# A two-layer encoder in fp32 halves: weight totals prepared by single transfers, and the first mixer weights split inside the down stage's written order

## The chip, the cores and the metric

The kernel runs on one core of one Trainium2 chip. The metric is the device time of one execution in microseconds (us). Three runs of the kernel before gave 2413.91 us as the median (2411.43 to 2414.56). The profiled execution is a fourth one and took 2415.7 us.

## The reference, cut to what matters

The input x has 512 tokens of 1024 features. Each of two layers adds half of a SwiGLU feed-forward network (FFN), then a mixer (a projection, three kinds of attention beside each other, gates, three branch projections and an output projection), then half of a second FFN. RMSNorm stands before each of the three, and once more at the end.

```python
for l in range(DEPTH):
    h = rms_norm(x, norm_g[l, 0])
    x = x + 0.5 * swiglu(h, ffn_w_gate[l, 0], ffn_w_up[l, 0], ffn_w_down[l, 0])
    h = rms_norm(x, norm_g[l, 1])
    proj = h @ w_in[l]
    ...
    x = x + merged @ w_o[l]
    h = rms_norm(x, norm_g[l, 2])
    x = x + 0.5 * swiglu(h, ffn_w_gate[l, 1], ffn_w_up[l, 1], ffn_w_down[l, 1])
return rms_norm(x, final_g)

def swiglu(h, w_gate, w_up, w_down):
    return (jax.nn.silu(h @ w_gate) * (h @ w_up)) @ w_down
```

## The kernel before, in words

**Halves.** Every fp32 operand of a matmul is split in two: a rounded high half, copied by ScalarE (ACT, `nc.scalar.copy`), and the rest, subtracted by VectorE (DVE). A product takes high by high, high by low and low by high. `weights` (L89) loads a 128x1024 weight tile over SyncE's queue (SP) into one of three `raw` buffers, splits it into one of four `whi` and `wlo` buffers, and then calls `ahead_by` (below). A `raw` buffer is free for the next load when the low half has been subtracted.

**FFN.** `ffn(l, i)` makes 22 tiles of 128 hidden features. The first ones are plain products. The other 20 run in `Seven`, which forms a block product of gate and up weights from seven half-sized products in place of eight. For this it needs sums of weight blocks, here called the weight totals: two 512 KB tiles for each of the 20 hidden tiles, `d_odd` (`t31`) and `d_even` (`t24`) in DRAM. FFN (0,0) makes what it needs on the way; for the FFNs (0,1), (1,0) and (1,1) the generator `prepare` makes them ahead of time with DMAs alone: two plain copies from ACT's queue, and three accumulating transfers from GpSimd's queue (POOL), of 512, 256 and 256 KB. That is 5 transfers per hidden tile and 100 per FFN. One step of the generator (one `yield`) issues the copies of tile k and the accumulating transfers of tiles k-2, k-4 and k-6, so up to 5 transfers at once.

**Pace.** `ahead_by(n)` adds n to a debt and takes one step of the generator for each whole unit of it. Each `weights` call adds `owed[1]`, which the stages set from `PACE`: the down stage (16 calls), the mixer's three parts (19, 22 and 25 calls). Each tile of `Seven` adds the value of `PACE["seven"]`. At its start, `ffn` calls `drained(l, i)`, which takes all steps that are still due for that FFN. `added` (L713) then reads the total of tile m, two tiles ahead of its use.

**Down stage.** `down` (L387) has eight output rows m. Rows 0 to 3 get plain products of hidden tiles 8 to 21; then four rounds j each make a seven-product of hidden tiles 0 to 7 for rows 2j and 2j+1, and plain products for row 4+j. `Operands` loads two weight rows; `first`, `second`, `third`, `fourth` split them or sums of them, `totals` and `more` make the sums on DVE. When a row is done, `advanced(m)` scales it (L491), adds it to x (L396), stores x, and lets ACT make the high half of the next norm's operand `h` (`begin`, L158); `completed(m)` makes its low half (L170) and sums the squares. The whole stage stands under `tiles.in_order()`: for each engine and queue, its instructions are chained in the order in which they are written.

**What sets the order elsewhere.** Outside of the chained blocks the framework's list scheduler orders each engine's instructions when the program is built, by readiness in its own timing and by place in the program; `tc.issue_after(ins)` adds an edge "behind this instruction in the engine's queue", without a wait. The engines run their queues in order. So the first weights of the mixer, w_qk (query and key of pair 0), then w_va, are split wherever the scheduler finds a free place in ACT's and DVE's queues between the last rows of the down stage. The mixer's first product (L119, L120, then L122) reads the eight tiles of `h` in order.

Of the kernel before, what the change touches and what calls it, by code (L numbers as in the profile page):

```python
# [2 lines left out]

# [1 line left out]

# [26 lines left out]
FOLD = 8  # L32
NO_WAIT = mybir.DependencyInfo(mybir.DependencyClass.NoSync, mybir.DependencyReason.DATA)
PACE = {
    "mixer": ((0.25, 0.45, 0.73), (0.12, 0.25, 0.43)),
    "seven": {(0, 1): 0.16, (1, 0): 0.15},
    "down": {(0, 0): 0.3, (0, 1): 0.47, (1, 0): 0.25},
}
LOW_FIRST = (2, 4, 7)
WIDE, WIDE_FIRST = frozenset((2, 3, 4, 5, 6, 7)), frozenset((3, 4, 5))  # L40
# [3 lines left out]
def encoder(ctx: ExitStack, tc: tile.TileContext, a: dict, out: bass.AP):  # L44
# [13 lines left out]
    def f(ap):  # L58
        return ap.bitcast(F32)
# [24 lines left out]


    loaded, lower, kept = [], [], []
    gbufs, whole, folded = [2 * (MF - FOLD)], {}, [True]
    prepared, ahead, due, owed, queue = {}, [], [], [0.0, 0.0], {}

    def weights(src, width=1024):  # L90
        raw = wpool.tile([P, 1024], F32, tag="raw", name="raw", bufs=3)
        hi = wpool.tile([P, 1024], F32R, tag="whi", name="whi")
        lo = wpool.tile([P, 1024], F32R, tag="wlo", name="wlo")
        for c in range(0, src.shape[-1], width):
            w = slice(c, min(c + width, src.shape[-1]))
            loaded[:] = [nc.sync.dma_start(raw[:, w], src[:, w]).ins]
            nc.scalar.copy(hi[:, w], raw[:, w])  # L97
            lower[:] = [nc.vector.tensor_tensor(out=lo[:, w], in0=raw[:, w], in1=f(hi[:, w]), op=ALU.subtract).ins]  # L98
        ahead_by(owed[1])
        return hi, lo  # L100

# [200 lines left out]
    def ffn(l, i, h, nxt=None):  # L302
# [4 lines left out]
        with tc.tile_pool(name="ffn", bufs=1) as fp, ExitStack() as order:  # L307
# [5 lines left out]
                order.enter_context(tc.issue_after(h.squared))  # L313
            else:
                sides = []
            drained(l, i)
            owed[1] = 0
            loads = []
            start, plain = (2, 4) if first else (0, 2)
# [61 lines left out]
            if nxt is None:  # L381
                finish(fp, ghi, glo, h, tiles)
                return
            owed[1] = PACE["down"].get((l, i), 0) * (1.5 if folded[0] else 1)
            down(l, i, h, nxt, fp, tiles, ghi, glo)

    def down(l, i, h, nxt, fp, tiles, ghi, glo):  # L387
# [7 lines left out]
        def add(out, in0, in1):  # L395
            nc.vector.tensor_tensor(out=out, in0=in0, in1=in1, op=ALU.add)  # L396
# [101 lines left out]
        def advanced(m):  # L498

            d, t = outs[m], xs[m]  # L500
            if m < KC - 1:
                nc.vector.scalar_tensor_tensor(
                    out=d, in0=d, scalar=-1.0 if m % 2 else 1.0, in1=banks[m], op0=ALU.mult, op1=ALU.add
                )
                scaled(d, d)
            else:
                scaled(d, banks[m])
            add(t, d, t)
            x_keep(m, t, nxt.step)
            nxt.begin(m, t)  # L510

        def squared(m):
            nxt.power(m, xs[m], lambda: fp.tile([P, S], F32, tag="sum", name="sq", bufs=2))
# [5 lines left out]
        with tiles.in_order():  # L519
# [32 lines left out]
            coming = Operands(1)  # L552
            sides.extend(folds)
            w22 = [fp.tile([P, S], F32R, tag="un", name="w22", bufs=FOLD) for _ in range(2)]
            w.first()
            w.totals()
            w.second()
            w.more()
            w.third()
            if l == i == 0:  # L560
                small_values()
            w.fourth()
            for j in range(KC // 2):
                m, last, parts = 4 + j, j == KC // 2 - 1, {}

                def begin():
                    parts[8] = split(m, 8, 8)

                def middle():
                    if j:  # L570
                        completed(2 * j - 1)
                    parts[16] = split(m, 16, 6)

                def late():
                    if not last:
                        coming.first()
                        coming.second()
                        coming.more()

                if not last:  # L580
                    coming.totals()
                added = seven(j, w, begin, middle, late)
                bank(m)
                plain(m, 8, parts[8])
                if last:
                    added()
                    advanced(2 * j)
                    squared(2 * j)
                    completed(2 * j)
                    d, t = outs[m], xs[m]  # L590
                    nc.vector.scalar_tensor_tensor(out=d, in0=d, scalar=-0.5, in1=h.rb, op0=ALU.mult, op1=ALU.mult)
                    add(t, d, t)
                    plain(m, 16, parts[16])
                    advanced(m)
                    squared(m)
                    completed(m)
                    continue
                coming.fourth()
                added()
                advanced(2 * j)  # L600
                coming.third()
                squared(2 * j)
                advanced(2 * j + 1)
                squared(2 * j + 1)
                completed(2 * j)
                plain(m, 16, parts[16])
                w, coming = coming, Operands(j + 2) if j < KC // 2 - 2 else None
# [104 lines left out]
    def added(l, i, m, fp, load=None):  # L712

        gu = a["w_gu"][l, i, m]
        with ExitStack() as order:
            if load is not None:
                order.enter_context(tc.issue_after(load))
            t = fp.tile([P, 2, S], F32, tag="sum", name="wsum", bufs=2)
            if (l, i) in prepared:
                loaded[:] = [nc.sync.dma_start(t, prepared[l, i][m][0]).ins]  # L720
                return t.rearrange("p n c -> p (n c)")
            loaded[:] = [nc.sync.dma_start(t, gu.rearrange("n p c -> p n c")[:, :, 0:S]).ins]
            t = t.rearrange("p n c -> p (n c)")
            nc.gpsimd.dma_start(t, gu[1], accum_op=ALU.add)
        return t

    def prepare(l, i):
# [5 lines left out]
        def flat(t):  # L733
            return t.rearrange("p n c -> p (n c)")
# [12 lines left out]
        for k in range(2, MF + 6):  # L747
            if k < MF:
                gu = a["w_gu"][l, i, k]
                t31, t24 = [  # L750
                    dram.tile([P, 2, S], F32, tag=f"d_{g}{l}{i}_{k}", name=f"d_{g}") for g in ("odd", "even")
                ]
                tiles[k] = t31, t24
                queued(nc.scalar.dma_start(t31, gu.rearrange("n p c -> p n c")[:, :, 0:S]))
                queued(nc.scalar.dma_start(flat(t24), gu[0]))
            if k - 2 in tiles:
                accumulate(flat(tiles[k - 2][0]), a["w_gu"][l, i, k - 2, 1])
            if k - 4 in tiles:
                t31, t24 = tiles[k - 4]
                accumulate(t24[:, 0], t31[:, 1])  # L760
            if k - 6 in tiles:
                t24 = tiles[k - 6][1]
                accumulate(t24[:, 1], t24[:, 0])
            yield

    def ahead_by(n):

# [4 lines left out]
                ahead.pop(0)  # L772
                due.pop(0)

    def drained(l, i):

        while (l, i) in due:
            if next(ahead[0], ahead) is ahead:
                ahead.pop(0)
                due.pop(0)  # L780
# [395 lines left out]
    def mixer(l, h, nxt):  # L1176
        with tc.tile_pool(name="mix", bufs=1) as mp:
# [1 line left out]


            def projected(c):
                w = weights(a["w_qk"][l, c])
                ps = mm_tile()
                product(ps, cols(w, KC), h.hi, h.lo)
                return ps
# [607 lines left out]
```

## Time and profile before

| what | before |
|---|---|
| median of three runs | 2413.91 us |
| profiled execution: its own time | 2415.7 us |
| profiled execution: span from first to last instruction | 2413.9 us |
| TensorE matmul (PE) busy | 99% |
| DVE, ACT, POOL busy | 76%, 57%, 15% |
| weight loads of PE (PEld) | 85% |
| mean granted TensorE clock | 0.996 |
| DMA traffic | 452.92 MB, mean 188 GB/s |
| chain that ended last | PE 90%, DVE 5%, DMA 2%, ACT 2%, issue 1% |

Times in the views are microseconds from the start of the span. A row of a timeline gives start, duration, engine, line and operation, output and input by name, shape, and how many instructions are merged; brackets give the idle time of the engine before it and what ended that idle time. Rows of waits give the waiting engine and line, what it waited for, then total, count and longest. The granted clock (PEclk) is 1.00 at 2.4 GHz and 0.50 at 1.2 GHz; a value between is a mean over the stretch.

### The profile page before, as it was taken

To read this page: it belongs to the slowest core of one execution; us is meant where nothing else is said; L and a number is where in the kernel's file an instruction comes from. 1 tells how busy PE (TensorE), PEld (TensorE's weight loads), DVE (VectorE), ACT (ScalarE), POOL (GpSimd) and SP (SyncE) were. 2 spreads that over 40 slices of the span, in tenths; PEclk is the share of its full clock that TensorE was granted. 3 is DMA by queue.
4 is the path that set the end of the run, shared out by engine and by line. 5 is a ranking of instruction groups with operands and counts; after the bars stand their busy time and mean duration, and the time that the engine had idled before them with its cause. 6 is when DMAs were issued, how large, how long until landed. Compare 5 with 4: busy or idle time off the path is not lost.

```text
span 2413.9 us, 35684 instructions
## 1 busy us (share of the span) xinstructions
PE 2385.9 (99%) x12954; PEld 2049.7 (85%) x12954; DVE 1832.0 (76%) x3328; ACT 1380.5 (57%) x2551; POOL 361.7 (15%) x524
## 2 busy tenths in 40 slices
PE   9999999999999999999999999999999999999998
PEld 7999888878888888887888888888888888888887
DVE  7999775756766779997889997767666666899832
ACT  6565545756666546664456664467566674566632
POOL 3100014422212110002100001143122100000000
PEclk9999999999999999999999999999999999999999
DMA  7675777687779766659556667565656824455532
GB/s 205 176 185 166 233 225 199 181 212 212 172 201 283 223 187 216 213 182 285 175 179 201 208 213 245 181 175 150 179 146 182 189 94 136 159 191 185 174 118 70
DMA packets 149777, 452.92 MB, mean 188 GB/s; under 512 B 18265, under 2 KB 23689, under 8 KB 148641
## 3 DMA queue, kind: packets, MB, share of 16 engines
q1 hardware_dynamic: 89856, 278.50, 34.7%
q0 software_dynamic: 40352, 107.36, 21.7%
q10 hardware_dynamic: 19392, 64.78, 7.5%
q8 instruction: 102, 1.67, 0.3%
q14 instruction: 75, 0.61, 0.1%
HBM read 428.52 MB, written 138.44 MB: 235 GB/s over the span
## 4 chain that ended last, share of the span: by engine, by line
PE 90%; DVE 5%; DMA 2%; ACT 2%; issue 1%; ACTq 0%; POOLq 0%; POOL 0%; DVEq 0%
PE mm L865 17%; PE mm L122 9%; PE pr L865 9%; PE mm L119 8%; PE mm L120 8%; PE plain L393 7%; PE pv L865 4%; PE mm L393 3%; PE mm L1570 2%; PE mm L1575 2%; PE mm L1571 2%; PE av L1357 2%; PE t L1347 1%; PE s L1302 1%; PE s L1303 1%; DVE wlo L106 1%
## 5 line engine op out<-in xcount | busy, mean ns | idle before, releaser
L98 DVE TENSOR_TENSOR wlo<-raw,whi 128x1024 fp32r<-128x1024 f32 x234 | 278.8, 1194 | 146.0 <-ACT whi L97 124.1
L97 ACT CAST whi<-raw 128x1024 fp32r<-128x1024 f32 x234 | 239.4, 1028 | 260.4 <-PE mm L120 89.1
L119 PE MATMUL mm<-h,whi 128*128 128x512 f32 x800 | 318.9, 399 | 4.3 <-ACT h L158 4.3
L120 PE MATMUL mm<-h,whi 128*128 128x512 f32 x800 | 314.9, 394 | 0.0
L122 PE MATMUL mm<-h,wlo 128*128 128x512 f32 x800 | 200.2, 393 | 0.6 <-DVE wlo L98 0.6
L106 DVE TENSOR_TENSOR wlo<-raw,whi 128x1024 fp32r<-128x1024 f32 x156 | 184.2, 1218 | 5.1 <-ACT whi L105 5.1
L122 PEld LDWEIGHTS mm<-h,wlo 128*128 128x128 f32 x800 | 151.8, 190 | 33.1 <-DVE wlo L98 1.0
L119 PEld LDWEIGHTS mm<-h,whi 128*128 128x128 f32 x800 | 150.4, 188 | 33.4 <-ACT h L158 5.1
L120 PEld LDWEIGHTS mm<-h,whi 128*128 128x128 f32 x800 | 150.8, 189 | 28.7
L393 PE MATMUL plain<-g,whi 128*128 128x512 f32 x672 | 162.0, 390 | 1.6 <-ACT whi L97 0.8
L105 ACT CAST whi<-raw 128x1024 fp32r<-128x1024 f32 x156 | 156.8, 1052 | 10.2 <-DMA raw<-in_w_gu 8.8
L393 PEld LDWEIGHTS plain<-g,whi 128*128 128x128 f32 x672 | 126.0, 188 | 30.3 <-DVE g L1005 1.6
L1316 ACT ACTIVATE lg<-lg,negm 128x256 f32<-128x256 f32 (+1 forms) x192 | 114.0, 594 | 27.0 <-DVE negm L1313 26.0
L105 ACT CAST whi<-wsum 128x1024 fp32r<-128x1024 f32 x90 | 94.8, 1053 | 41.5 <-PE pv L865 32.6
L984 ACT COPY gu<-mm 128x512 f32<-128x512 f32 (+1 forms) x78 | 41.9, 538 | 131.2 <-PE mm L865 131.2
L106 DVE TENSOR_TENSOR wlo<-wsum,whi 128x1024 fp32r<-128x1024 f32 x90 | 109.5, 1216 | 6.3 <-ACT whi L105 4.4
L901 DVE TENSOR_TENSOR gu<-pr,gu 128x256 f32<-128x256 f32 x234 | 98.2, 420 | 9.7 <-ACT gu L939 5.6
L67 POOL DMA_DIRECT2D x<-d_x x24 | 13.4, 558 | 561.1 <-DVE gu L901 493.7
L745 POOL DMA_DIRECT2D d_odd<-in_w_gu x60 | 51.1, 856 | 306.9 <-DMA d_odd<-in_w_gu 189.2
L1558 DVE TENSOR_TENSOR z<-mm,rb 128x512 f32<-128x512 f32 x48 | 33.1, 691 | 76.4 <-PE mm L122 76.3
L865 PEld LDWEIGHTS mm<-h,whi 128*128 128x128 f32 x624 | 83.7, 189 | 5.6 <-PE st L247 0.4
L865 PE MATMUL mm<-h,whi 128*128 128x256 f32 x624 | 86.9, 281 | 0.0
(361 smaller groups left out, 6205.7 us busy)
## 6 DMA issues: line engine op xcount, KB each, us to landing
raw<-in_w_gu SPq DMA_DIRECT2D x94, 512.0 KB, 3.4
d_odd<-in_w_gu ACTq DMA_DIRECT2D x60, 512.0 KB, 5.9
d_even<-in_w_gu ACTq DMA_DIRECT2D x60, 512.0 KB, 6.6
d_odd<-in_w_gu POOLq DMA_DIRECT2D x60, 512.0 KB, 8.9
wsum<-d_odd SPq DMA_DIRECT2D x60, 512.0 KB, 3.2
raw<-d_even SPq DMA_DIRECT2D x60, 512.0 KB, 4.4
raw<-in_w_gate SPq DMA_DIRECT2D x48, 512.0 KB, 5.3
raw<-in_w_qk SPq DMA_DIRECT2D x44, 512.0 KB, 5.1
```

Of the source, the lines that this page charges most:

```text
L97: nc.scalar.copy(hi[:, w], raw[:, w])
L98: lower[:] = [nc.vector.tensor_tensor(out=lo[:, w], in0=raw[:, w], in1=f(hi[:, w]), op=ALU.subtract).ins]
L105: nc.scalar.copy(hi, src)
L106: nc.vector.tensor_tensor(out=lo, in0=src, in1=f(hi), op=ALU.subtract)
L119: nc.tensor.matmul(ps, wh, xhi[k], start=k == 0, stop=False)
L120: nc.tensor.matmul(ps, wh, xlo[k], start=False, stop=False)
L122: nc.tensor.matmul(ps, wl, xhi[k], start=False, stop=k == n - 1)
L393: nc.tensor.matmul(ps, w, x, start=start, stop=stop, skip_group_check=True)
L745: queued(nc.gpsimd.dma_start(out, more, accum_op=ALU.add, max_dma_last_dim=4 * 1024))
L865: nc.tensor.matmul(out, wk, bk, start=go, stop=end, skip_group_check=True)
L901: nc.vector.tensor_tensor(out=out, in0=in0, in1=in1, op=ALU.add)
L1316: nc.scalar.activation(p, p, AF.Exp, bias=negm, scale=-1.0, accum_out=total)
```

## The change

**Preparing.** `prepare` yields after each single transfer, so a unit of pace is now one transfer. All values of `PACE` are new, and the down stage has two (rows 0 to 3, and the four rounds). The former factor of 1.5 in the down stage goes. `ready[l, i]` notes the last tile whose totals have been issued, and `drained(l, i, m)` moves from the start of the FFN into `added`: it takes only as many transfers as tile m still lacks.

**Seam to the mixer.** In the last round of the down stage of the first FFN of each layer (`i == 0`), the loads and splits of the two w_qk tiles are written into the chained order, behind `completed(6)`; the mixer's first two projections take them from `begun`. `completed(6)` itself moves behind two DVE instructions of row 7. `advanced` now returns its add, and in both FFNs that have a down stage the next two `weights` calls put their DVE subtraction behind the add of row 7 (`guard`).

**First round.** `w.totals()` (two DVE adds) is written ahead of `w.first()` (a split on ACT and DVE).

```diff
 PACE = {
-    "mixer": ((0.25, 0.45, 0.73), (0.12, 0.25, 0.43)),
-    "seven": {(0, 1): 0.16, (1, 0): 0.15},
-    "down": {(0, 0): 0.3, (0, 1): 0.47, (1, 0): 0.25},
+    "mixer": ((1, 1, 1.9), (0.6, 0.8, 1.2)),
+    "seven": {(0, 1): 2, (1, 0): 2},
+    "down": {(0, 0): (1, 2.75), (0, 1): (0.4, 1.5), (1, 0): (1, 2.5)},
 }
...
             nc.scalar.copy(hi[:, w], raw[:, w])
-            lower[:] = [nc.vector.tensor_tensor(out=lo[:, w], in0=raw[:, w], in1=f(hi[:, w]), op=ALU.subtract).ins]
+            with tc.issue_after(guard.pop()) if guard else nullcontext():
+                lower[:] = [nc.vector.tensor_tensor(out=lo[:, w], in0=raw[:, w], in1=f(hi[:, w]), op=ALU.subtract).ins]
...
-            drained(l, i)
             owed[1] = 0
...
-            owed[1] = PACE["down"].get((l, i), 0) * (1.5 if folded[0] else 1)
+            owed[1] = PACE["down"].get((l, i), (0, 0))[0]
...
+            w.totals()
             w.first()
-            w.totals()
             w.second()
...
             w.fourth()
+            owed[1] = PACE["down"][l, i][1]
...
                     squared(2 * j)
-                    completed(2 * j)
                     d, t = outs[m], xs[m]
                     nc.vector.scalar_tensor_tensor(out=d, in0=d, scalar=-0.5, in1=h.rb, op0=ALU.mult, op1=ALU.mult)
                     add(t, d, t)
+                    completed(2 * j)
+                    if i == 0:
+                        begun.extend(weights(a["w_qk"][l, c]) for c in range(2))
                     plain(m, 16, parts[16])
-                    advanced(m)
+                    guard[:] = 2 * [advanced(m)]
...
             if (l, i) in prepared:
+                drained(l, i, m)
                 loaded[:] = [nc.sync.dma_start(t, prepared[l, i][m][0]).ins]
...
                 queued(nc.scalar.dma_start(t31, gu.rearrange("n p c -> p n c")[:, :, 0:S]))
+                yield
                 queued(nc.scalar.dma_start(flat(t24), gu[0]))
+                yield
             if k - 2 in tiles:
                 accumulate(flat(tiles[k - 2][0]), a["w_gu"][l, i, k - 2, 1])
+                yield
             if k - 4 in tiles:
                 t31, t24 = tiles[k - 4]
                 accumulate(t24[:, 0], t31[:, 1])
+                yield
             if k - 6 in tiles:
                 t24 = tiles[k - 6][1]
                 accumulate(t24[:, 1], t24[:, 0])
-            yield
+                ready[l, i] = k - 6
+                yield
...
-        while (l, i) in due:
+        while (l, i) in due and ready.get((l, i), 0) < m:
...
-                w = weights(a["w_qk"][l, c])
+                w = begun.pop(0) if begun else weights(a["w_qk"][l, c])
```

## Rows read from the trace of the kernel before

**Rows 1.** The page, its first part: busy time, share, instructions of each engine.
```profile
PE 2385.9 (99%) x12954; PEld 2049.7 (85%) x12954; DVE 1832.0 (76%) x3328; ACT 1380.5 (57%) x2551; POOL 361.7 (15%) x524
```
**Rows 2.** Waits of PE over the whole span: total us, times, longest.
```profile
PE t L1442 <- DVE lg L1503: 4.5, 1, 4.5
PE mm L119 <- ACT h L158: 4.3, 2, 2.3
PE mm L393 <- ACT gu L468: 1.8, 1, 1.8
PE mm L393 <- DVE wlo L106: 1.5, 1, 1.5
...
PE plain L393 <- ACT whi L97: 0.8, 1, 0.8
```
**Rows 3.** Windows behind long PE waits: us, engines' busy (instructions), PEclk, DMA share, GB/s.
```profile
357.50:362.00 4.50, 4.50 (x13) 3.55 (x14) 1.30 (x2) 1.49 (x2) 0.14 (x1) 0.62 0.69 230
...
1556.30:1560.90 4.60, 4.60 (x13) 3.69 (x14) 1.34 (x2) 1.51 (x2) 0.10 (x1) 0.63 0.52 175
...
527.60:535.00 7.40, 7.40 (x25) 6.04 (x26) 2.75 (x5) 2.68 (x5) 0.00 (x0) 0.66 0.36 127
```
**Rows 4.** Timeline of DVE at the seam from down stage to mixer, layer 0.
```profile
345.11 0.69 DVE L396 TENSOR_TENSOR x<-gu,x 128x512 f32<-128x512 f32 x1
...
352.31 1.22 DVE L98 TENSOR_TENSOR wlo<-raw,whi 128x1024 fp32r<-128x1024 f32 x1
353.45 0.68 DVE L396 TENSOR_TENSOR x<-gu,x 128x512 f32<-128x512 f32 x1
354.24 0.69 DVE L491 SCALAR_TENSOR_TENSOR gu<-plain,rb 128x512 f32<-128x512 f32 x1
354.85 1.22 DVE L98 TENSOR_TENSOR wlo<-raw,whi 128x1024 fp32r<-128x1024 f32 x1
355.98 0.69 DVE L396 TENSOR_TENSOR x<-gu,x 128x512 f32<-128x512 f32 x1
```
**Rows 5.** Timeline of ACT at the same seam.
```profile
351.64 1.05 ACT L97 CAST whi<-raw 128x1024 fp32r<-128x1024 f32 x1 [0.71 <-DMA raw<-in_w_va]
...
356.70 0.72 ACT L158 ACTIVATE h<-x,ng 128x512 fp32r<-128x512 f32 x1 [4.01 <-DVE x L396]
```
**Rows 6.** Timeline of PE at the same seam.
```profile
350.29 1.52 PE L393 MATMUL plain<-g,wlo 128*128 128x512 f32 x6
351.65 0.39 PE L119 MATMUL mm<-h,whi 128*128 128x512 f32 x1
...
357.47 0.73 PE L119 MATMUL mm<-h,whi 128*128 128x512 f32 x2 [2.04 <-ACT h L158]
```
**Rows 7.** Chain of waits, down stage of FFN (0,1): start, us, what.
```profile
1089.20 12.09 DMA d_odd<-in_w_gu
...
1106.18 16.71 DMA raw<-in_w_down
```
**Rows 8.** DMA issues, same stage, 1085 to 1135: count, KB, median us to landing.
```profile
raw<-in_w_down SPq DMA_DIRECT2D x3, 512.0 KB, 16.3
```
**Rows 9.** DMA issues at the seam, 337 to 352.
```profile
raw<-in_w_va SPq DMA_DIRECT2D x3, 512.0 KB, 9.2
```
**Rows 10.** DMA issues in Seven of FFN (0,1), 1030 to 1070: no preparing transfers.
```profile
raw<-in_w_gu SPq DMA_DIRECT2D x4, 512.0 KB, 3.3
```
**Rows 11.** DMA issues in the same stage, 948 to 968: one step of five.
```profile
raw<-in_w_gu SPq DMA_DIRECT2D x2, 512.0 KB, 6.7
```
**Rows 12.** Windows of that stage, with the step and without; columns as in rows 3.
```profile
950.00:970.00 20.00, 19.48 (x120) 17.11 (x119) 17.83 (x32) 12.67 (x21) 2.51 (x3) 1.00 0.92 284
...
1030.00:1050.00 20.00, 20.00 (x126) 17.96 (x125) 19.24 (x33) 13.49 (x23) 0.00 (x0) 1.00 0.54 184
```
**Rows 13.** Timeline of PE in the stretch with the step.
```profile
965.29 1.20 PE L865 MATMUL mm<-pair,whi 128*128 128x512 f32 x4 [0.52 <-ACT gu L933]
```
**Rows 14.** Timeline of DVE in the mixer of layer 0, ahead of the long wait.
```profile
521.89 1.22 DVE L98 TENSOR_TENSOR wlo<-raw,whi 128x1024 fp32r<-128x1024 f32 x1 [9.58 <-ACT whi L97]
```

More of the change, by code (lines that the diff above doesn't have):

```diff
@@ L1 @@
 import math
-from contextlib import ExitStack, contextmanager
+from contextlib import ExitStack, contextmanager, nullcontext
 import numpy as np
@@ L86, in encoder @@
     loaded, lower, kept = [], [], []
+    begun, guard = [], []
     gbufs, whole, folded = [2 * (MF - FOLD)], {}, [True]
-    prepared, ahead, due, owed, queue = {}, [], [], [0.0, 0.0], {}
+    prepared, ready, ahead, due, owed, queue = {}, {}, [], [], [0.0, 0.0], {}
     def weights(src, width=1024):
@@ L507, in advanced @@
                 scaled(d, banks[m])
-            add(t, d, t)
+            row = nc.vector.tensor_tensor(out=t, in0=d, in1=t, op=ALU.add).ins
             x_keep(m, t, nxt.step)
             nxt.begin(m, t)
+            return row
         def squared(m):
@@ L773, in ahead_by, with drained @@
                 due.pop(0)
-    def drained(l, i):
-        while (l, i) in due:
+    def drained(l, i, m):
+        while (l, i) in due and ready.get((l, i), 0) < m:
             if next(ahead[0], ahead) is ahead:
```

## The prediction

> **What bounds the kernel now.** I read the first part of the page, then PE's waits, then the windows behind the long ones, and only then the timelines. PE is busy for 2385.9 of the span's 2413.9 us [rows 1]. The change adds and removes no matmul, so what it can win is in PE's idle time, about 28 us, and in the clock that such idle time costs. The waits say where that is [rows 2]. One transpose waits 4.5 us for a softmax. Twice, 4.3 us together, the first product of a mixer waits for `h` (L158): the seam behind the down stage, once per layer. Three waits of 1.8, 1.5 and 0.8 us stand in a down stage. The rest are short ones that the change does not touch, or the program's start.
>
> A long wait costs more than itself. Behind each seam and behind the transpose the granted clock is at its lower level of 1.2 GHz for a while, which shows as a mean below 1 [rows 3]: 0.62 over 4.50 us, 0.63 over 4.60 us, 0.66 over 7.40 us. Busy time at a mean of 0.62 does 0.62 of the work, so the loss is 0.38 x 4.50 = 1.7 us, 0.37 x 4.60 = 1.7 us and 0.34 x 7.40 = 2.5 us. PE did nothing in the wait just before each. Behind the three waits in the down stage the clock stays up.
>
> **The seams.** In layer 0 PE ends the last row at about 351.8 (350.29 + 1.52), has begun the mixer at 351.65, and stops at 355.4, until `h` of row 7 comes at 357.47: 2.04 us [rows 6]. Of that `h`, ACT waits 4.01 us for DVE's add [rows 5]. DVE shows why [rows 4]: two subtractions for mixer weights, 1.22 us each, stand among the instructions of row 7, at 352.31 and 354.85. The first one pushes the scaling (L491) to 354.24 though the row is ready at 351.8; the second stands between it and the add (355.98).
>
> With the change both are behind the add. Then the scaling can begin at 351.9, the add at about 352.6, `h` at 353.3, and it ends at 354.0 (0.69 + 0.69 + 0.72, with the small steps between). When does PE need it? The first product starts at 351.65, and seven tiles of `h` give it 14 high-weight matmuls. Six matmuls of that size start between 350.29 and 351.65 [rows 6], 0.23 us each, so 14 take 3.2 us: 354.8. The wait should go, with 0.8 us to spare. What is late next is the low half of the same tile on DVE, which a pinned subtraction of 1.22 us can precede; I leave 0.3 us per seam for it. The w_qk splits that the change moves cost nothing as long as they fit into the last row's products. On DVE they take 2.44 us, and PE's last row is behind them.
>
> Per seam: 2.04 + 1.7 in layer 0, and in layer 1 4.3 - 2.04 = 2.3 plus 1.7. Together 7.7, less 0.6: **-7.1 us**. Bounds: 0 if another late thing takes its place (first rival), -7.7.
>
> The other seam, from FFN (0,1) to FFN (1,0), has the pin too, but no long wait stands there in rows 2: 0.
>
> **The down stage of FFN (0,1).** The chain runs for 12.09 us through one preparing copy, and then for 16.71 us through one load of down weights [rows 7]; the loads of this stretch land 16.3 us after issue [rows 8], against 3.3 us for a load of the same size in a calm stretch [rows 10]. By the code, a step was due every 1/0.705 calls there, up to five transfers at once: 23 transfers in the first eight calls. After the change these calls owe 0.4 each: 4 transfers. With 19 fewer transfers the loads should land nearly as in the calm. The waits of 0.8, 1.5 and 1.8 us are all late weights in that stage, so **-4.1 us**. Bounds: -4.1 and 0. The new order of the sums and the first split helps in the same place and has nothing left to win once the rows are early; on its own I put it at 0, since DVE does the same instructions and the adds only change places with a subtraction.
>
> **Where the transfers go.** All 300 stay. My count of the debt by stage, before and after: down (0,0) 23 and 30, with 5 more in the two moved calls; mixer of layer 0 130 and 85; Seven of (0,1) 15 and 40; down (0,1) 32 and 16; Seven of (1,0) 7 and 39; down (1,0) 26 and 28, with 5 more; mixer of layer 1 67 and 52. FFN (1,0) now starts with 76 of its 100, which makes tiles up to 12 ready, and runs ahead of need by the pace of 2; the forced part of `drained` is never taken. So no total is late by the count, and the reads two tiles ahead hide the landing.
>
> The two Seven stages get denser: two transfers in each tile. A tile is about 9.8 us long, by the distance at which its rows return in the timeline. Five transfers raised the DMA share from 0.54 to 0.92 over 20 us [rows 12], which is 7.6 us of all engines, 1.5 us each. Two per tile add 3.0 us in 9.8: 0.54 + 0.31 = 0.85. There is room, but less. With the five, the weight load took 6.7 us in place of 3.3 [rows 10, 11], and PE waited 0.52 us [rows 13]. Bounds: 0, and 0.52 us in each tile that gets an accumulating transfer, which is 4 of 5 tiles, 32 in all: +16.6. Two transfers are nearer to none than to five, and in a tile where only the two copies fell PE waited for nothing; I take **+1 us**.
>
> The Trainium skill, "DMA: Bandwidth & Descriptors", section "Issuing engines are not separate DMA queues", speaks against a free gain here: transfers started from the ACT, SP and POOL queues all run on the same 16 DMA engines and interleave, so an even pace moves contention and removes none. The rise of the load's landing from 3.3 to 6.7 us agrees with it. By that rule the Seven stages pay for what the down stage gains, which is the third rival below.
>
> **The mixers.** Outside the chained blocks the scheduler's order will shift, because the preparing transfers sit elsewhere in ACT's and POOL's queues. The stall of 4.5 us in layer 0 is such an order: DVE stood 9.58 us behind one weight subtraction [rows 14], with the softmax queued behind it. It can go (-4.5 - 2.5 = -7.0) and a like one can come (+7.0). I take 0.
>
> **Sum.** -7.1 - 4.1 + 1 = -10.2. The span of 2413.9 becomes 2403.7, and the profiled execution's 2415.7 about 2405.5. That execution lay 1.8 us above the median of the runs, 2413.91; from this median the forecast is 2404. A difference under 0.2%, 4.8 us, can't be told from none.
>
> **Rivals.**
>
> *The seam stays, with another cause.* On ACT a split of w_va that waits for its load can stand ahead of row 7's `h`, as one does in the trace at 351.64 [rows 5]; the pin holds only DVE's half. There are three `raw` buffers, so the load of the second w_va tile waits until the first w_qk tile is subtracted, and that now stands behind row 6. Row 6's add ends at 345.8 [rows 4]; add 0.72 for `h`, about 0.7 for its squares on ACT, 1.05 and 1.22 for the split: 349.5. A load landing in 3.3 us [rows 10] comes at 352.8, ACT is free at 353.9 and `h` is done at 354.6: nothing lost. One that takes 9.2 us, as the w_va loads do here [rows 9], comes at 358.7, `h` at 360.5, and PE waits 5.7 us in place of 2.0. Between the ends, at 5 to 6 us, the seam costs what it costs now. Then only the down stage gains: -4.1 + 1, 2411. For it: the loads at this seam are slow, and 5 transfers fall into the two moved calls. Against: whether the scheduler puts the split first is open.
>
> *The mixer's long wait goes too.* 2404 - 7 = 2397. For it: the order that made it depends on the pace, and rows 2 show just one wait of this kind for two mixers of the same code. Against: no part of the change aims there.
>
> *The Seven stages saturate, and it gets slower.* If an accumulating transfer per tile makes the weight loads as late as five did, 32 tiles lose 0.52 us: -11.2 + 16.6, 2419. It decides from the point where the load lands near 6.7 us in the common tile. Against: 0.85 is below the 0.92 of that stretch, and the load is issued a tile ahead.
>
> *The pace does not do what it says:* transfers still bunch, since ACT's and POOL's queues are held up by other work; down (0,1) keeps its waits, and only the seams gain: 2414 - 7, 2407.
>
> **How the numbers follow.** Forecast 0.42, seam stays 0.25, mixer wait goes 0.13, Seven saturates 0.12, pace without effect 0.08. The likeliest case gives 2404, and with its own bounds 2400 to 2408. The range takes in the second and third cases with their unknown mixer order: 2394 to 2419. Faster by over 0.2% (below 2409.1): 0.42 and 0.13 almost whole, most of 0.08, less what a new wait in a mixer takes back, 0.57. Slower by over 0.2% (above 2418.7): half of the 0.12, and the seam case with a long load or a new mixer wait, 0.15. Same: 0.28.
>
> **What would show it.** PE's waits: L119 for `h` gone or below 0.5 us at both seams, with PEclk near 1 behind them; on DVE no L98 between L491 and L396 of row 7. In the down stage of FFN (0,1) the weight loads land in under 8 us and the three waits are gone. In the Seven stages the share is near 0.85 and waits of L865 sum to under 2 us. I am wrong if ACT shows an L97 waiting for w_va ahead of the last L158, if many tiles of Seven wait 0.5 us, or if a mixer has a new wait of several us.

## The result and the profile after

After the change the kernel takes 2421.4 us (median; 2418.5 to 2423.8) against 2414.1 us before in the same session: a ratio of 1.0029, 95% interval 1.0018 to 1.0040. It is slower by 7 us where 10 us less were forecast, and lies above the range. The profiled execution took 2423.0 us, its span is 2421.3 us.

The amount of work on TensorE is as before; the first part of the page of the kernel after, against [rows 1]:

```profile
PE 2387.4 (99%) x12954; PEld 2051.6 (85%) x12954; DVE 1835.0 (76%) x3328; ACT 1380.3 (57%) x2551; POOL 367.3 (15%) x524
```

So the 7 us are in waits again, and in the clock behind them. PE's waits of the kernel after (what waited for what: total us, times, longest), against [rows 2]:

```profile
PE mm L121 <- ACT h L160: 11.7, 2, 7.5
PE pr L876 <- DVE wlo L108: 4.6, 2, 4.5
PE mm L876 <- ACT gu L944: 3.1, 6, 1.5
PE mm L1082 <- ACT whi L1041: 1.7, 1, 1.7
```

The waits for the softmax (4.5) and in the down stage (1.8, 1.5, 0.8) are gone. The waits for `h` at the two seams, which the change was forecast to remove, have grown from 4.3 to 11.7 us, and one of 4.5 us is new. Timeline of PE of the kernel after: the end of row 7's products and where the three long waits end (against [rows 6]); then the windows behind these waits, with the granted clock (columns as in [rows 3]):

```profile
351.38 1.52 PE L394 MATMUL plain<-g,wlo 128*128 128x512 f32 x6
...
363.53 0.80 PE L121 MATMUL mm<-h,whi 128*128 128x512 f32 x1 [7.46 <-ACT h L160]
...
1238.09 0.79 PE L876 MATMUL pr<-pair,wlo 128*128 128x256 f32 x2 [4.48 <-DVE wlo L108]
...
1562.97 0.80 PE L121 MATMUL mm<-h,whi 128*128 128x512 f32 x1 [4.23 <-ACT h L160]
```
```profile
360.00:366.80 6.80, 3.27 (x7) 2.29 (x8) 2.49 (x3) 3.23 (x4) 0.00 (x0) 0.50 0.61 210
1237.20:1244.00 6.80, 5.91 (x20) 5.23 (x21) 4.05 (x6) 2.98 (x7) 0.00 (x0) 0.50 0.89 263
1561.50:1568.30 6.80, 5.33 (x13) 4.22 (x14) 2.49 (x3) 2.98 (x4) 0.00 (x0) 0.50 0.98 327
```

At 0.50 (1.2 GHz) a busy microsecond does half its work, so half of PE's busy time in these windows is lost: 1.6, 3.0 and 2.7 us. That gives the balance, after less before, in the prediction's own terms (wait plus clock):

| place | before | after | difference | forecast |
|---|---|---|---|---|
| seam to the mixer, layer 0 | 2.0 + 1.7 | 7.5 + 1.6 | +5.4 | -3.4 |
| seam to the mixer, layer 1 | 2.3 + 1.7 | 4.2 + 2.7 | +2.9 | -3.7 |
| start of FFN (1,0) | 0 | 4.5 + 3.0 | +7.5 | 0 |
| rest of Seven (waits of its matmul for gu) | 1.3 | 3.1 | +1.8 | +1 |
| opening, first 50 us (without the 1.5 us at its start that both have) | 1.1 | 2.0 + 1.7 | +2.6 | 0 |
| down stage of FFN (0,1) | 4.1 | 0 | -4.1 | -4.1 |
| mixer of layer 0 | 4.5 + 2.5 | 0 | -7.0 | 0 |
| sum | | | +9.1 | -10.2 |

The clock's part in the opening is a mean of 0.57 over 8 to 12 us, with PE busy for all 4.00 us; the kernel before has 1.00 there. The spans differ by 7.4 us, so the balance is 1.7 us too large, and where those are lost it does not show.

**Why `h` is late.** Timelines of DVE and then of ACT of the kernel after at the seam of layer 0, against [rows 4, 5]:

```profile
349.31 0.69 DVE L397 TENSOR_TENSOR x<-gu,x 128x512 f32<-128x512 f32 x1 [2.42 <-DMA x<-in_xT]
...
351.18 2.35 DVE L100 TENSOR_TENSOR wlo<-raw,whi 128x1024 fp32r<-128x1024 f32 x2
353.45 0.69 DVE L492 SCALAR_TENSOR_TENSOR gu<-plain,rb 128x512 f32<-128x512 f32 x1
354.17 0.69 DVE L509 TENSOR_TENSOR x<-gu,x 128x512 f32<-128x512 f32 x1
```
```profile
361.81 1.05 ACT L98 CAST whi<-raw 128x1024 fp32r<-128x1024 f32 x1 [10.21 <-DMA raw<-in_w_va]
362.76 0.72 ACT L160 ACTIVATE h<-x,ng 128x512 fp32r<-128x512 f32 x1
```

DVE does nearly as forecast: the scaling and the add stand back to back, and row 7 is done at 354.9, 2.0 us after its products (351.38 + 1.52 = 352.9). The two w_qk subtractions ahead of the scaling end 0.6 us after the products and hold it up by that much. Then nothing happens to it for 8 us, because the next instruction in ACT's queue is a weight copy for w_va (L98), which waits for its load, and `h` (L160) is written behind it. The chain of waits of the kernel after (start, us, what) tells why that load is late:

```profile
340.65 8.53 DMA x<-in_xT
...
351.26 1.15 DVE wlo L100
...
352.43 9.31 DMA raw<-in_w_va
```

The load needs a `raw` buffer, which comes free with a w_qk subtraction (L100). That subtraction is now chained behind `completed(6)`, and this behind the first add into row 7 (L397 at 349.31), which waits 2.42 us for row 7's tile of x; that tile took 8.53 us to land. The load itself then takes 9.31 us, as in [rows 9]. In layer 1 no tile of x is late (the load goes out 3.8 us after row 6's add), and the same load takes 9.36 us.

**Start of FFN (1,0).** Chain of waits of the kernel after:

```profile
1208.89 1.13 DVE wlo L100
...
1211.29 1.15 DVE wlo L100
...
1212.46 5.20 DMA raw<-in_w_gu
...
1226.03 1.13 DVE wlo L100
...
1227.19 7.40 DMA raw<-d_even
...
1236.82 1.23 DVE wlo L108
1238.09 1.01 PE pr L876 x3
```

The pin (`guard`) at this seam puts the subtractions of two gate and up weights behind row 7's add (1208.2); the buffers come free late, a load of weights goes out only at 1212.46, and the load of a total (`d_even`), which needs the next buffer, only at 1227.19, 19.0 us after the add began. In the trace before the same add began at 1214.52, and the load of the total was issued 3.8 us later:

```profile
1218.29 0.43 SPq L841 DMA_DIRECT2D raw<-d_even  x1
```

The late load then takes 7.40 us. From 1222 to 1240 the packets of POOL's queue, which carries the accumulating transfers, take 78.7% of the DMA engines' time. Which part is the pin's and which the transfers' is seen in seam_only below.

**What went right.** Loads of down weights in the down stage of FFN (0,1) of the kernel after (count, KB, median us to landing), against [rows 8]; and the windows of Seven against [rows 12]:

```profile
raw<-in_w_down SPq DMA_DIRECT2D x4, 512.0 KB, 7.1
```
```profile
950.00:970.00 20.00, 20.00 (x123) 17.91 (x122) 18.81 (x33) 12.79 (x21) 2.50 (x3) 1.00 0.94 271
1030.00:1050.00 20.00, 20.00 (x126) 17.96 (x125) 19.21 (x34) 13.58 (x23) 0.00 (x0) 1.00 0.70 238
```

7.1 us in place of 16.3, and no wait of PE is left there.

### The profile page after: what moved, and what is told of

Its sections match the earlier page's. It is cut to its first block, busy times and chain, and to the rows that moved or that the text cites. A ratio compares the mean times of both kernels' runs of the same rounds, so it can differ in the third digit from the quotient of the medians.

```text
span 2421.3 us, 35674 instructions
## 1 busy us (share of the span) xinstructions
PE 2387.4 (99%) x12954; PEld 2051.6 (85%) x12954; DVE 1835.0 (76%) x3328; ACT 1380.3 (57%) x2551; POOL 367.3 (15%) x524
## 4 chain that ended last, share of the span: by engine, by line
PE 90%; DVE 5%; DMA 2%; ACT 2%; issue 1%; SPq 0%; POOLq 0%; ACTq 0%; POOL 0%; DVEq 0%
PE mm L876 17%; PE plain L394 9%; PE mm L124 9%; PE pr L876 8%; PE mm L121 8%; PE mm L122 8%; PE pv L876 4%; PE mm L394 3%; PE av L1368 2%; PE mm L1586 2%; PE mm L1581 2%; PE mm L1582 2%; PE t L1358 1%; PE s L1313 1%; PE s L1314 1%; DMA raw<-in_w_gu 1%
## 5 line engine op out<-in xcount | busy, mean ns | idle before, releaser
L98 ACT CAST whi<-raw 128x1024 fp32r<-128x1024 f32 x234 | 239.2, 1027 | 252.3 <-PE mm L122 84.2
L100 DVE TENSOR_TENSOR wlo<-raw,whi 128x1024 fp32r<-128x1024 f32 x234 | 280.5, 1201 | 128.2 <-ACT whi L98 108.1
L121 PE MATMUL mm<-h,whi 128*128 128x512 f32 x800 | 319.6, 400 | 11.7 <-ACT h L160 11.7
L876 PE MATMUL mm<-pair,whi 128*128 128x512 f32 (+1 forms) x384 | 86.0, 353 | 3.1 <-ACT gu L944 3.1
```

The costliest lines, as they stand in the source:

```text
L121: nc.tensor.matmul(ps, wh, xhi[k], start=k == 0, stop=False)
L876: nc.tensor.matmul(out, wk, bk, start=go, stop=end, skip_group_check=True)
```

## The experiments

The theory, "order": on ACT a copy that waits for its load stands ahead of row 7's `h`, in the mixer's seam, and at the seam between the FFNs the pinned subtractions (the pin is the `guard`) hold the load buffers. Rivals: "buffer" and "density" (the load is late by itself, and with an early load the order is harmless), "pace" (the new pace costs it all). Medians, each against the kernel before of the same session (the ratios are those on record and not always the quotient of the two medians):

| run | us | before | ratio, 95% |
|---|---|---|---|
| act_pin | 2409.5 | 2413.9 | 0.9982 (0.9971 to 0.9992) |
| pin_mixer_only | 2416.9 | 2413.9 | 1.0013 (1.0003 to 1.0023) |
| both_mended | 2404.1 | 2413.9 | 0.9965 (0.9952 to 0.9978) |
| pace_only | 2418.6 | 2413.9 | 1.0020 (1.0011 to 1.0028) |
| seam_only | 2418.0 | 2412.5 | 1.0014 (1.0005 to 1.0023) |
| sparse_seam | 2410.7 | 2412.5 | 0.9993 (0.9984 to 1.0002) |
| early_begun | 2406.4 | 2412.5 | 0.9963 (0.9951 to 0.9976) |
| seven_held | 2403.7 | 2412.5 | 0.9952 (0.9940 to 0.9965) |
| pace_held | 2418.1 | 2412.9 | 1.0021 (1.0009 to 1.0032) |
| early_held | 2403.1 | 2412.9 | 0.9956 (0.9943 to 0.9968) |
| seven_free | 2408.6 | 2414.9 | 0.9968 (0.9957 to 0.9978) |
| seven_plain | 2407.9 | 2414.9 | 0.9969 (0.9958 to 0.9980) |

**act_pin**: the kernel after, with ACT's half of the two pinned splits queued behind row 7's `h` as well (`begin` returns its instruction, `advanced` both).

```diff
-            nc.scalar.copy(hi[:, w], raw[:, w])
-            with tc.issue_after(guard.pop()) if guard else nullcontext():
+            row, high = guard.pop() if guard else (None, None)
+            with tc.issue_after(high) if high else nullcontext():
+                nc.scalar.copy(hi[:, w], raw[:, w])
+            with tc.issue_after(row) if row else nullcontext():
```

> The changed kernel with one addition: ACT's half of the next two weight splits behind a down stage (L98) is queued behind row 7's h, as the pin already does with DVE's half. The transfers and their pace stay. Theory 'order': PE's long waits at both seams (7.5 and 4.2 us for h) come from a w_va split that stands ahead of that h on ACT and waits for its load; with it behind, h is made about 0.7 us after row 7's add and both waits fall under 0.5 us, and the low clock behind them goes: 9.8 and 7.1 us of loss fall to about 0.6 each, 2421.4 - 15.7 = about 2406 us. Rival 'density': the seam is late because loads and x tiles land late beside dense preparing transfers, whatever stands first on ACT; then waits of 4 us or more stay and the time stays above 2418 us.

2409.5, 12 us under the kernel after, where about 2406 was expected. Timeline of ACT at the seam:

```profile
352.91 0.72 ACT L162 ACTIVATE h<-x,ng 128x512 fp32r<-128x512 f32 x1 [4.93 <-DVE x L511]
...
359.25 1.05 ACT L100 CAST whi<-raw 128x1024 fp32r<-128x1024 f32 x1 [4.15 <-DMA raw<-in_w_va]
```

`h` comes right after the add, the copy waits for its load behind it, and PE waits for `h` at neither seam. Two waits stay in FFN (1,0). One of 3.6 us at 1201.7 is at the pinned seam; both_mended drops the pin there, and this wait with it. One of 2.3 us at 1293.7 is in Seven, behind a weight load of 10.49 us, and is of the kind that seven_plain is about.

**pin_mixer_only**: the kernel after, with the pin only where a mixer follows.

```diff
-                    guard[:] = 2 * [advanced(m)]
+                    row = advanced(m)
+                    guard[:] = 2 * [row] if i == 0 else []
```

> The changed kernel without the pin at the seam from FFN (0,1) to FFN (1,0); the pin at the two mixer seams stays. Theory 'pin holds buffers': there the pinned DVE halves keep two of the three raw buffers until row 7 is done, so the weights behind them and the first d_even total load late, and PE waits 4.5 us at 1238 us with the low clock behind; without the pin this wait is under 0.5 us and the time falls by about 7 us, 2421.4 to about 2414 us. Rival 'late totals': the wait comes from accumulating transfers that bunch at the start of this Seven stage and delay the d_even load; then it stays at 3 us or more and the time stays near 2421 us.

2416.9, where about 2414 was expected. The wait of 4.5 us is gone (the longest between 1200 and 1300 is 1.0 us), the seams to the mixers keep 12.4 us. By the medians that is 4.5 us, by the two profiled spans 9.8 us; this kernel's runs spread over 9 us (2412.9 to 2421.9), so the price of this pin is known only as 4 to 10 us.

**both_mended**: both edits.

> Both edits: ACT's half pinned too, and the pin at the two mixer seams only. If both theories hold, the gains add up: 2421.4 - 15.7 - 7.3 = about 2398 us, below the kernel before by 0.65%. If only the order at the mixer seams counts, about 2406 us; if only the buffers at the other seam count, about 2414 us; if neither, 2421 us.

2404.1: 17.3 us below the kernel after and 0.35% below the kernel before, though 6 above what was expected of the run. PE's waits, for comparison with the four lines above, and the windows of the two seams:

```profile
PE mm L1264 <- DVE qn L1210: 2.7, 2, 1.4
PE mm L1084 <- ACT whi L1043: 2.4, 1, 2.4
```
```profile
350.00:400.00 50.00, 48.40 (x220) 39.57 (x219) 28.86 (x42) 20.37 (x33) 16.29 (x25) 1.00 0.90 255
...
1550.00:1600.00 50.00, 48.60 (x231) 40.02 (x230) 30.42 (x61) 28.63 (x57) 19.86 (x26) 1.00 0.66 194
```

No wait for `h` is left at these two seams (one of 1.3 us stands at the seam between the FFNs, where the kernel before has none), and the clock stays up. PE is idle for 1.6 and 1.4 us in these windows, 3.0 together. In the trace before it is idle there for 4.3 and loses 0.03 x 48 = 1.4 us in each to the clock: 7.2. So the seams, mended, gain 4.2 us, not 7.1: next late at both is `qn`, a result that DVE makes for the mixer (L1264, 2.7 us together). The two mended places account for the miss in size (17.3 of 17); that the time equals the forecast's is chance, since the mixer's -7.0 makes up for what the seams and the opening (L1084, 2.4) fall short.

**seam_only**: the kernel before with the new seam and first round, and the old `prepare` and `PACE`. **pace_only**: the kernel after with the old seam.

> The kernel before with the seam edits and the new first round alone: splits pulled forward and pinned, old preparing and old pace. If the seam edits do harm by themselves, the waits for h are 4 us or more at the mixer seams and there is a wait of some us at the start of Seven in FFN (1,0), since the pin holds raw buffers there too: 2416 to 2424 us. If they do harm only beside the denser transfers, the waits for h are at most those of the kernel before (2.0 and 2.3 us) and the time is 2414 us or less.

> The preparing by single transfers with the new pace, the readiness tile by tile and the new order of the first round, with the seams written as before (no splits pulled forward, no pin). Theory 'the seam edits did the harm': the waits for h are near those of the kernel before (2.0 and 2.3 us), no wait at 1238 us, the waits of the down stage of FFN (0,1) are gone (-4 to -5 us), the mixer's own wait of 4.5 us may go or stay: 2402 to 2410 us. Rival 'density did the harm': with 5 more transfers near each mixer seam the waits for h grow to 4 us or more also without the seam edits, and the time is 2414 us or more.

seam_only is slower than before by itself; its timeline of ACT at the seam has the same two rows, with the old pace:

```profile
357.59 1.04 ACT L98 CAST whi<-raw 128x1024 fp32r<-128x1024 f32 x1 [9.34 <-DMA raw<-in_w_va]
358.54 0.72 ACT L160 ACTIVATE h<-x,ng 128x512 fp32r<-128x512 f32 x1
```

PE waits 5.7 us (layer 0) and 3.2 us for `h` there, and the waits of the down stage stay. So the loss at the seams to the mixers needs no new pace. At the start of FFN (1,0) it is otherwise (PE's wait there, as above):

```profile
PE pr L870 <- DVE wlo L108: 0.8, 2, 0.7
```

The pin is the same, and the load of the total goes out as late as in the kernel after (1231.01, 19.5 us after row 7's add began), but it lands in 3.3 us in place of 7.40, and PE waits 0.7 us where some us were expected. So the 4.5 us there take the pin and the new transfers together; taking away either one leaves no wait above 1.0 us there.

pace_only missed its expectation: its down stage is free of waits, but in Seven two new ones of 3.9 and 4.4 us stand (at 912.7 and 1258.2), and the waits for `h` are 3.1 and 2.6 us, a little more than before. The mixer's wait of 4.5 us is gone in both, with the old pace in one and the old seam in the other. Both have the new order of the first round, and no run leaves that out, so which edit removed this wait is not shown.

**sparse_seam**: the kernel after, without preparing transfers in the last round of the two down stages that precede a mixer (`if last and i == 0: owed[1] = 0`). **early_begun**: the kernel after, with the w_qk loads and splits written one place earlier.

```diff
                         coming.more()
+                    elif i == 0:
+                        begun.extend(weights(a["w_qk"][l, c]) for c in range(2))
...
                     completed(2 * j)
-                    if i == 0:
-                        begun.extend(weights(a["w_qk"][l, c]) for c in range(2))
```

> The changed kernel without preparing transfers in the last round of the down stages of FFN (0,0) and (1,0), the two moved calls included (debt 0 there; the later stages take them over). The order on ACT stays as it is. Theory 'order, with density as its size': the w_va split still stands ahead of row 7's h, but its load lands in 3 to 5 us instead of 9.3 and row 7's x tile is in time, so the load goes out about 350 us and lands at 353 to 355; the waits for h shrink from 7.5 and 4.2 us to 0 to 2 us: about 2409 to 2414 us. If order alone counted, the waits would stay above 4 us (2419 us or more); if density alone, they would be gone.

> The changed kernel with the two w_qk loads and splits written earlier in the last round: ahead of its seventh block product, not behind row 6. The pin and the pace stay, ACT's halves are not pinned. Theory 'buffer': the second w_va load waits for the raw buffer of the first w_qk tile, so it goes out at 352.4 us and lands at 361.7; with the split some 9 us earlier it goes out at about 343, lands by 352 to 353, ACT's split is over before row 7's add, and both waits for h fall under 1 us: 2421.4 - 13 = about 2408 us (the wait of 4.5 us at 1238 us stays). Rival 'density': the landing of 9 us is what counts wherever the split stands; the waits stay at 3 us or more and the time above 2416 us.

Timeline of ACT at the seam, sparse_seam and then early_begun:

```profile
352.99 1.06 ACT L98 CAST whi<-raw 128x1024 fp32r<-128x1024 f32 x1 [3.49 <-DMA raw<-in_w_va]
353.94 0.72 ACT L160 ACTIVATE h<-x,ng 128x512 fp32r<-128x512 f32 x1
```
```profile
354.38 1.05 ACT L98 CAST whi<-raw 128x1024 fp32r<-128x1024 f32 x1 [2.18 <-DMA raw<-in_w_va]
355.33 0.72 ACT L160 ACTIVATE h<-x,ng 128x512 fp32r<-128x512 f32 x1
```

In both the copy still stands ahead of `h`. In sparse_seam the load landed in 3.8 us in place of 9.31 and nobody waits; in early_begun it still took 12.1 us, but went out at 342.20 in place of 352.43, and PE waits 1.2 us. So the three theories are three factors of one wait: the order makes it possible, the buffer sets when the load starts, the density how long it takes (and, by the late tile of x, the start as well: in sparse_seam the load went out at 349.13). Taking away any one leaves 1.2 us of wait for `h` at most. In sparse_seam Seven's waits grow to 5.2 us. The wait of 4 us at the start of FFN (1,0) stays in both, as the pin there does.

**seven_held, pace_held, early_held**: both_mended, pace_only and early_begun (with pin_mixer_only's edit) with Seven's `ahead_by` call moved into the chained block.

```diff
-            ahead_by(PACE["seven"].get(self.at, 0))
+                ahead_by(PACE["seven"].get(self.at, 0))
```

> The kernel with both seams mended (2404 us), and the preparing transfers of each Seven tile written inside its chained order, so that none can be issued before its tile's turn. Theory 'bunching': a new unit of one transfer has nothing that holds it to its tile, accumulating transfers run ahead on POOL in bunches, and a weight load beside them lands after 10 us instead of 3.3, for which PE waits now and then; held to their tiles, the waits of the Seven stages of FFN (0,1) and (1,0) fall below 1 us together, runs scatter less, and the time is 2400 to 2403 us. Rival 'two per tile are too many': evenly spread they still make loads late, waits of 0.3 to 0.5 us appear in many tiles, and the time is 2405 us or more.

> The new preparing and pace with the seams as before (2418.6 us without this edit), and the transfers of each Seven tile written inside its chained order. In the run without it, PE waited 4.0 us at 912 and 4.6 us at 1258 us, each behind a weight load of more than 10 us, and lost 5.5 and 7 us in these stretches with the low clock. Theory 'bunching': held to their tiles, no load of these stages takes more than about 7 us, both waits fall under 1 us, and the time falls by 9 to 12 us to 2407 to 2410 us. Rival 'two per tile are too many': the waits move to other tiles or spread over many, and the time stays above 2415 us.

> The changed kernel with the w_qk splits written ahead of the seventh product (2406.4 us), the pin at the two mixer seams only, and the Seven transfers held to their tiles; ACT's halves not pinned. The wait of 3.9 us at the start of Seven in FFN (1,0), with its low clock some 7 us, should go: 2399 to 2402 us, equal to or a little below the mended kernel with held transfers (2403.7 us). If the pin there was not the cause in this arrangement, 2405 to 2407 us.

The edit was to spread the accumulating transfers, and did not: they still leave POOL's queue in threes. pace_held keeps its two waits and missed its expectation; seven_held is no different from both_mended, and its waits for `gu` are 3.5 us in all against 2.3. Of the cause of Seven's waits these three say nothing. early_held is rid of the 4 us at the start of FFN (1,0), as expected, and with 2403.1 stays 1 us above its forecast; it is with seven_held and both_mended the best of the study, at 0.35 to 0.48% below the kernel before.

**seven_free, seven_plain**: pace_only, with Seven's accumulating transfers left out, or sent as plain copies of the same sizes on the same queue. `quiet` is set while Seven's tiles take their steps. The plain copies also go without `max_dma_last_dim`, the limit on a row's length.

```diff
         def accumulate(out, more):
-            queued(nc.gpsimd.dma_start(out, more, accum_op=ALU.add, max_dma_last_dim=4 * 1024))
+            if quiet[0]:
+                queued(nc.gpsimd.dma_start(out, more))
+            else:
+                queued(nc.gpsimd.dma_start(out, more, accum_op=ALU.add, max_dma_last_dim=4 * 1024))
```

> The new pace with the old seams, and in the two Seven stages that prepare, the accumulating transfers on POOL's queue are left out (their copies on ACT's queue stay; the totals they would have completed are wrong). New pace alone is at 2418.6 with waits of 3.9 us near 912 and 4.4 us near 1258 in Seven. If transfers in a bunch make these waits (theory 'bunch'), both fall under 1 us, no weight load there lands later than about 6 us, and the time falls by 7 to 10, to 2408 to 2411. If the waits come from the order of the loads and splits (rival 'order'), a wait of 3 us or more stays in one of the Seven stages and the time stays above 2414.

> As the one before, but the same transfers are kept as plain copies on the same queue, same sizes, without the addition (the totals are wrong there). If it is the addition that makes a transfer hold the DMA engines long (theory 'accumulating'), the waits in Seven fall under 1.5 us each and the time falls to 2409 to 2412. If any bunch of three DRAM-to-DRAM transfers does it (rival 'density'), waits of 3 us or more stay and the time is 2416 to 2420.

Chain of waits of pace_only ahead of its second wait:

```profile
1244.60 10.75 DMA raw<-in_w_gu
...
1256.32 1.04 ACT whi L107
...
1258.20 1.22 PE mm L874 x2
```

Timeline of POOL, pace_only and then seven_plain, at the same tile:

```profile
1242.30 0.80 POOL L749 DMA_DIRECT2D d_odd<-in_w_gu  x1 [11.07 <-DMA d_odd<-in_w_gu]
1242.89 1.05 POOL L749 DMA_DIRECT2D d_even<-d_odd  x1
1243.41 1.38 POOL L749 DMA_DIRECT2D d_even<-d_even  x1
```
```profile
1239.66 0.50 POOL L751 DMA_DIRECT2D d_odd<-in_w_gu  x1 [19.64 <-DMA d_odd<-in_w_gu]
1240.31 0.53 POOL L751 DMA_DIRECT2D d_even<-d_odd  x1
1240.83 0.52 POOL L751 DMA_DIRECT2D d_even<-d_even  x1
```

Both send three at once. (The head of the queue waits for a copy, and the two behind it follow.) PE's waits, whole span, pace_only, seven_plain and seven_free:

```profile
PE mm L874 <- ACT gu L942: 9.1, 6, 4.4
```
```profile
PE mm L878 <- ACT gu L946: 2.0, 5, 1.1
```
```profile
PE mm L876 <- ACT gu L944: 0.9, 4, 0.4
```

As plain copies the three are harmless: 10.7 us less time (2418.6 to 2407.9), as much as leaving them out. So it is neither the bunch nor the bytes: of the two weight loads of the stretch 1236 to 1259 the median lands in 7.1 us beside accumulating transfers, 5.2 beside plain ones, 3.3 beside none. What it is about an accumulating transfer stays open, because the edit takes away the addition and the row limit together, and the same three transfers then go in fewer packets (POOL's queue from 895 to 914 us, pace_only and then seven_plain: packets, MB, the time that they took as a share of 16 engines):

```profile
q0 software_dynamic: 432, 1.05, 35.2%
```
```profile
q0 software_dynamic: 192, 1.05, 17.8%
```

## Why the prediction was wrong

**The seams: this step failed.** "The wait should go, with 0.8 us to spare" priced what DVE does, and DVE did it, to the row: no subtraction stands between scaling and add. The add ends 2.0 us after the products, where 1.5 was reckoned, because the w_qk subtractions, put at no cost, run 0.6 us past the products. What the sum left out is that ACT, where `h` is made, has a queue too, and only DVE's half was pinned. The first rival had the mechanism, the copy ahead of `h`, the late buffer, the 9 us load, and even a price of 5.7 us of wait at the far end; but it was costed at "what it costs now". The runs put it at 7.5 and 4.2 us plus clock, +8.3 us together in place of -7.1. Two reasons: in both layers the load does take 9.3 us, the row that [rows 9] had shown, not the 5 to 6 at which the wait would have broken even; and in layer 0 it started at 352.4, not 349.5. The rival's sum has the w_qk split right behind row 6, but the change also moves `completed(6)`, and the split with it, behind the first add into row 7, which waited for its tile of x. In seam_only, where that tile was in time, the wait in layer 0 is the rival's 5.7 us. The price was to be taken from the row for this very load, not from the calm one. act_pin and both_mended show that with the copy behind `h` the wait goes as forecast, and that 4.2 of the 7.1 us are then gained.

**The other seam: this step failed too.** That it "has the pin too, but no long wait stands there in rows 2: 0" was read from what waits before the change. Where nothing waits, a pin can only add a wait, and here it did, together with the denser transfers: 4.5 us and 3.0 of clock, against 0.7 us with the old pace (seam_only). What was to be asked is who needs the pinned instruction's result: the freed buffer, and with it the loads behind it. pin_mixer_only removes that wait.

**The down stage of FFN (0,1): right.** -4.1 forecast, the three waits gone, loads at 7.1 us ("under 8").

**Seven: right in the kernel after, by luck of phase.** +1 was forecast and +1.8 came, with a share of 0.94 and 0.70 in the two windows where 0.85 was worked out for all tiles: the transfers still go in bunches. In pace_only the same pace cost two waits of 4 us and more, which is the third rival in another form: not 0.5 us in every tile, but two bad tiles. In the one shown the load was issued right behind the accumulating three, and seven_plain shows that the same bytes as plain copies do no such harm. The rule in the Trainium skill ("DMA: Bandwidth & Descriptors", section "Issuing engines are not separate DMA queues"), that all queues' transfers interleave on the same engines, agrees with the loads' rise. It gives no price by the kind of transfer, and here the kind decides: 7.1 us for a load beside accumulating ones, 5.2 beside plain copies of the same bytes.

**The mixer: the second rival.** Its -7.0 came true, in seam_only and pace_only as well; which edit changed that order is not shown, since every run has the new first round. It was rightly not in the sum: nothing in the profile fixes its sign. It hid half of the loss; without it the change would have measured some 14 us slower.

**Left open:** why a wait of L1082 (1.7 us), with a low clock behind it, came up in the opening, the exact price of the second pin, which edit took away the mixer's wait, and whether it is the addition or the number of packets that makes the accumulating transfers dear.

## What to carry to other kernels

Pin an operation on every engine that has a part of it, or find out which queue the late result really comes from: an instruction that waits for a load blocks all that is written behind it on its engine. Where a buffer is freed by an instruction that you move back, the next load moves back with it, so cost the move at the load's own measured time in that stretch, and where the pin stands a second time, cost it there too, even if nothing waits there now, and with the load times that the rest of the change will make. A wait with several factors can be removed at the cheapest of them; here an earlier load, a calmer stretch and an order on ACT each did.

## What the runs showed of the hardware

Accumulating DRAM transfers, as this kernel cuts them, cost weight loads more than plain copies of the same bytes: with them a 512 KB load issued right behind three of them took 10.75 us, and the three themselves 6.3 (512 KB), 9.0 and 12.3 us (256 KB each); as plain copies on the same queue they took 5.4, 7.0 and 7.4 us. Another three of the same sizes took 35.2% of the engines' time over 19 us in 432 packets, and 17.8% in 192 packets as plain copies. A full DMA window is not in itself a loss: in both_mended the share stands at 0.97 from 358 to 366 us, with PE busy throughout and the granted clock at 1.00.
